# Output projection and second MLP product: from feature-major to token-major

## The chip, the cores and the metric

The kernel runs on one core of a Trainium2 chip. The metric is the device time of one execution in microseconds (us); the median of several runs is compared. A profiled execution gives the trace: when each instruction ran on each engine and what it waited for. PE is the matrix engine (TensorE), DVE the vector engine, ACT the scalar engine, POOL is GpSimd; SP issues the DMAs.

## The reference

Two layers of a hybrid block on 512 tokens x and 256 context tokens ctx, with D = 1024. A modulation vector of c (and of c_ctx) gives, per layer, shifts, scales and gates. A token mixer has three branches (a convolution over 31 tokens, a bidirectional mLSTM in chunks of 128, a latent attention with 8 heads). Their gated sum goes through the output projection. Then come a layer norm, an MLP with 4096 hidden features and a second layer norm:

```python
def layer_norm(x, g, b):
    mu = jnp.mean(x, -1, keepdims=True)
    var = jnp.mean(jnp.square(x - mu), -1, keepdims=True)
    return (x - mu) * lax.rsqrt(var + LN_EPS) * g + b

# per layer l, alpha = 4 ** 0.25
u = x * (1.0 + sc1) + sh1
y = (g_a * y_a + g_b * y_b + g_c * y_c) @ w_out[l] + b_out[l]
x = layer_norm(alpha * x + g1 * y, ln1_g[l], ln1_b[l])
x = layer_norm(alpha * x + g2 * sq_relu_mlp(x * (1.0 + sc2) + sh2, w1[l], b1[l], w2[l], b2[l]), ln2_g[l], ln2_b[l])
```

where sq_relu_mlp(u) = square(relu(u @ w1 + b1)) @ w2 + b2. In the first layer the 256 context tokens go through the same steps with their own modulation; in the second they only feed keys, values and states. The result is x, 512 x 1024.

## The kernel before

All activations lie feature-major: 128 features on the partitions, tokens along the free dimension (T = 768: 512 of x, then 256 of ctx; in the second layer only n = 512 are carried through the mixer's output and the MLP). A token tile tt is 128 tokens.

**Products.** `gemm` (L279) computes one tile of 128 output features. Its stationary operands are 128 x 128 blocks of the weight, its moving operand is the activation, 512 tokens and then 256. Each product is done three times (`mm3`, L265), as float32 in two halves: `wh` and `wl` of the weight (high part and rest), and likewise for the activation: h*h, h*l, l*h. The sum stands in `pg`, one of two PSUM buffers of two banks each; `gemm_parts` (L292) takes `pt`, of which there are four of one bank each.

**Weights.** `plan` (L201) lists all weight chunks (128 x 1024, 512 KB) in the order of use. `wget` (L249) hands out the next and stages two more: a DMA on SP's queue into `wr`, ACT casts it into `wh` (L261), DVE (for some chunks POOL) subtracts into `wl` (L262). There are three buffers of each.

**Order.** Only the first stage is written out by hand. After it the framework sets each engine's order when the program is built, earlier text first where several instructions are ready, so PE's work of a later step fills waits of an earlier one.

**Slots.** `slot` gives one of 35 general SBUF buffers of 128 x 768; `vp` has 12 buffers (vectors of attention and mLSTM, later `t1`), `mp` ("m") has 8 of 128 x 512.

**Output projection and first norm** (L1098 to L1107). The tokens go in groups of 256, `tg_`: three in layer 0, two in layer 1. Per group all eight chunks of w_out are loaded again; each output tile is multiplied by its gate and added to the residual (L1104), which came by DMA and an ACT scaling (`residual`, L1085). Then `ln_groups` (L304): for each token tile, eight PE transposes bring it to rows (L314), DVE takes mean and variance (L315 to L322, the power -0.5 on POOL, L321), ACT norms from PSUM (L326), and PE transposes each of the eight feature tiles back (L336) to `norm1` (L1074), which makes the MLP's input `u2` (scale and shift per feature on DVE, L1080; cast on ACT; rest on POOL, L1082) and, on ACT, the start value of the MLP's accumulator `acc` (L1083).

**MLP** (L1113 to L1141). Eight blocks f: four tiles of the first product with relu and square (L1126 to L1129), then, except in the last block, eight tiles of the second product, each with four k; DVE multiplies by the gate and adds into `acc` (L1139). The first two tiles and each block's last one are done in parts of 256 tokens (`split_spec`), so that they can start when one group is ready. In layer 0, `pull` (L346) also feeds in the next layer's modulation (L165, DVE).

**Last block and second norm.** `last_w2` (L1148) does the last block's second product per group of 256 and loads its four chunks for each; then the norm follows as above. In layer 0 `norm2` (L1160) makes the next layer's input u and stores the normed x feature-major; in layer 1 the rows are scaled by rows of ln2's weights (L1191, L1192, on DVE and POOL) and stored.

Layer 1's first products (`win`, L468) read u with 512 tokens at a time.

## Time and profile before

| | us |
|---|---|
| median of 3 runs | 2556.21 (2555.85 to 2561.79) |
| the profiled execution | 2557.35 |
| its span, first to last instruction | 2555.5 |

| engine | busy us | share | instructions |
|---|---|---|---|
| PE (matmul) | 2470.4 | 97% | 15272 |
| PE (weight load) | 2163.8 | 85% | 15272 |
| DVE | 1580.6 | 62% | 2847 |
| ACT | 939.5 | 37% | 1607 |
| POOL | 298.7 | 12% | 235 |

The granted TensorE clock was 0.993 of full speed. The stages, by the trace's own clock: in layer 0 the output projection runs from about 888 us, the MLP from 965, its last product from 1478; layer 1 begins at about 1525 and has them from 2130, 2180 and 2515.

How to read it: busy times are those of one execution. Matmuls are pipelined, so the time of one (0.39 us for 512 columns) is longer than the distance from one start to the next; what PE spends on one is read from starts in the timeline. "idle <- X" names what ended an engine's wait. The kernel lines (L266) are those of the kernel before; a helper's line stands for all its callers, and the tile names (pg<-zp) tell which.

### The profile page before, as it was taken

To read this page: it belongs to the slowest core of one execution; us is meant where nothing else is said; L and a number is where in the kernel's file an instruction comes from. 1 tells how busy PE (TensorE), PEld (TensorE's weight loads), DVE (VectorE), ACT (ScalarE), POOL (GpSimd) and SP (SyncE) were. 2 spreads that over 40 slices of the span, in tenths; PEclk is the share of its full clock that TensorE was granted. 3 is DMA by queue.
4 is the path that set the end of the run, shared out by engine and by line. 5 is a ranking of instruction groups with operands and counts; after the bars stand their busy time and mean duration, and the time that the engine had idled before them with its cause. 6 is when DMAs were issued, how large, how long until landed. Compare 5 with 4: busy or idle time off the path is not lost.

```text
span 2555.5 us, 38339 instructions
## 1 busy us (share of the span) xinstructions
PE 2470.4 (97%) x15272; PEld 2163.8 (85%) x15272; DVE 1580.6 (62%) x2847; ACT 939.5 (37%) x1607; POOL 298.7 (12%) x235
## 2 busy tenths in 40 slices
PE   7899989999999999999999999999999999999997
PEld 5888878888888899888888888977888888888887
DVE  4999976363356777655554379996043567554456
ACT  3123323222457563222222253333324575432323
POOL 0002132203000021000000031023411001100002
PEclk9999999999999999999999999999999999999999
DMA  7122344466110654343342252233563106333333
GB/s 264 53 75 70 98 163 161 166 195 210 62 34 1 188 168 142 122 131 115 108 129 88 65 149 78 59 106 101 175 203 111 50 18 213 101 99 92 99 94 113
DMA packets 137235, 298.45 MB, mean 117 GB/s; under 512 B 13776, under 2 KB 55248, under 8 KB 137056
## 3 DMA queue, kind: packets, MB, share of 16 engines
q1 hardware_dynamic: 137056, 296.00, 36.9%
q8 instruction: 120, 1.97, 0.3%
q14 instruction: 59, 0.48, 0.1%
HBM read 265.49 MB, written 30.46 MB: 116 GB/s over the span
## 4 chain that ended last, share of the span: by engine, by line
PE 81%; DVE 9%; DMA 4%; ACT 2%; issue 2%; POOL 1%; SPq 0%; DVEq 0%; ACTq 0%; POOLq 0%
PE pg L266 21%; PE pg L267 21%; PE pg L268 21%; PE pt L1003 2%; PE pt L982 2%; PE pt L266 2%; PE pt L267 2%; PE pt L268 2%; DVE ca L494 2%; DMA wm<-w_mod 1%; DMA ml<-z_dram 1%; PE pg L536 1%; PE pg L538 1%; PE pg L537 1%; DVE st L315 1%
## 5 line engine op out<-in xcount | busy, mean ns | idle before, releaser
L261 ACT CAST wh<-wr 128x1024 fp32r<-128x1024 f32 (+1 forms) x328 | 345.6, 1055 | 1202.4 <-PE pg L267 825.5
L262 DVE TENSOR_TENSOR wl<-wr,wh 128x1024 fp32r<-128x1024 f32 (+2 forms) x272 | 338.6, 1246 | 410.1 <-ACT wh L261 406.3
L268 PE MATMUL pg<-uh,wl 128*128 128x512 f32 (+1 forms) x1280 | 456.3, 356 | 2.2 <-DVE wl L262 2.2
L266 PE MATMUL pg<-uh,wh 128*128 128x512 f32 (+1 forms) x1280 | 457.2, 357 | 1.2 <-ACT gt__17278 L760 1.2
L267 PE MATMUL pg<-ul,wh 128*128 128x512 f32 (+1 forms) x1280 | 455.5, 356 | 0.7 <-POOL ul L1171 0.6
L266 PE MATMUL pg<-hidh,wh 128*128 128x512 f32 (+1 forms) x832 | 285.4, 344 | 3.9 <-DVE mv L318 2.0
L267 PE MATMUL pg<-hidl,wh 128*128 128x512 f32 (+1 forms) x832 | 284.9, 342 | 0.0
L268 PE MATMUL pg<-hidh,wl 128*128 128x512 f32 (+1 forms) x832 | 284.2, 342 | 0.0
L266 PEld LDWEIGHTS pg<-uh,wh 128*128 128x128 f32 x1280 | 244.2, 191 | 35.4 <-issue 2.5
L268 PEld LDWEIGHTS pg<-uh,wl 128*128 128x128 f32 x1280 | 243.9, 191 | 34.4 <-DVE wl L262 2.7
L267 PEld LDWEIGHTS pg<-ul,wh 128*128 128x128 f32 x1280 | 244.1, 191 | 33.2 <-POOL ul L1171 1.0
L494 DVE SCALAR_TENSOR_TENSOR ca<-hc,cols,ca 128x511 f32<-128x511 f32 (+9 forms) x360 | 227.8, 673 | 2.4
L262 POOL TENSOR_TENSOR wl<-wr,wh 128x1024 fp32r<-128x1024 f32 x56 | 145.7, 2602 | 562.6 <-ACT wh L261 562.6
L267 PE MATMUL pg<-u2l,wh 128*128 128x512 f32 (+1 forms) x608 | 210.3, 347 | 0.3 <-POOL u2l L1082 0.2
L1139 DVE SCALAR_TENSOR_TENSOR acc<-pg,mod,acc 128x512 f32<-128x512 f32 (+1 forms) x168 | 106.0, 659 | 168.6 <-PE pg L268 168.6
L268 PE MATMUL pg<-u2h,wl 128*128 128x512 f32 (+1 forms) x608 | 210.1, 347 | 0.0
L266 PE MATMUL pg<-u2h,wh 128*128 128x512 f32 (+1 forms) x608 | 209.9, 347 | 0.0
L165 DVE SCALAR_TENSOR_TENSOR mda<-wm,sil,mda 128x512 f32<-128x512 f32 x224 | 176.2, 808 | 7.6 <-DMA wm<-w_mod 5.0
L266 PEld LDWEIGHTS pg<-hidh,wh 128*128 128x128 f32 x832 | 157.3, 190 | 25.3 <-issue 3.5
L321 POOL TENSOR_TENSOR rs<-rs,mhalf 128x1 f32<-128x1 f32 x30 | 24.4, 819 | 1298.5 <-DVE rs L320 1298.5
L267 PEld LDWEIGHTS pg<-hidl,wh 128*128 128x128 f32 x832 | 157.9, 190 | 18.7 <-DVE hidl L1129 1.6
L268 PEld LDWEIGHTS pg<-hidh,wl 128*128 128x128 f32 x832 | 157.7, 189 | 18.0
(359 smaller groups left out, 4754.1 us busy)
## 6 DMA issues: line engine op xcount, KB each, us to landing
wr<-w SPq DMA_DIRECT2D x140, 512.0 KB, 3.6
wr<-w_in_fm SPq DMA_DIRECT2D x104, 512.0 KB, 3.8
wm<-w_mod SPq DMA_DIRECT2D x192, 256.0 KB, 4.5
wr<-w_out SPq DMA_DIRECT2D x40, 512.0 KB, 3.9
ml<-z_dram SPq DMA_DIRECT2D x104, 128.0 KB, 2.8
ml<-z_dram SPq DMA_DIRECT2D x48, 256.0 KB, 4.4
z_dram<-ml SPq DMA_DIRECT2D x32, 256.0 KB, 4.5
dm<-m_dram SPq DMA_DIRECT2D x20, 256.0 KB, 4.4
```

The lines of the kernel that those rows point to most:

```text
L165: ins = V.scalar_tensor_tensor(av[v], w, sil[:, k, v:v + 1], av[v], op0=OP.mult, op1=OP.add)
L261: A.copy(h[:, :n], r[:, :n])
L262: eng.tensor_sub(lo[:, :n], r[:, :n], h[:, :n])
L266: PE.matmul(ps, hs, xh, start=first, stop=False)
L267: PE.matmul(ps, hs, xl, start=False, stop=False)
L268: return PE.matmul(ps, ls, xh, start=False, stop=last)
L315: V.bn_stats(st[:, hf * 6:(hf + 1) * 6], ps)
L494: V.scalar_tensor_tensor(acc[:, a:b], h[:, a + d:b + d], wd(15 + d), acc[:, a:b], op0=OP.mult, op1=OP.add)
L536: PE.matmul(o, uh[:, t0:t0 + 128], wh[:, a:b], start=(k == 0), stop=False)
L982: PE.transpose(p2[:, y * 128:(y + 1) * 128], P[:, (k4 + y) * 128:(k4 + y + 1) * 128], ident)
L1003: PE.matmul(po[64 * i:64 * i + 64, :256], va[B_.k0 + k][:, h * 64:h * 64 + 64], B_.pts[i][k // 2][:, k % 2, :], start=(k == 0), stop=(k == ...
L1139: V.scalar_tensor_tensor(acc[mt][:, c0:c1], ps[:, c0:c1], mc[:, 40 + mt, v:v + 1], acc[mt][:, c0:c1], op0=OP.mult, op1=OP.add)
```

## The change

Output projection and second MLP product are computed with tokens on the partitions: 128 tokens of the activation are the stationary operand, 512 output features of the weight the moving one. Each token tile has two halves (hf) of 512 features, each in one PSUM bank. Tokens go in two groups, `tri`: three tiles each in layer 0 (the second is tiles 3, 4, 5, that is the last of x and both of ctx), two each in layer 1. The weights of w_out and w2 are packed accordingly, and are loaded twice (w_out, and w2's last block) where they were loaded three times in layer 0.

Gates, biases and residual scales, which were per partition, become rows of 1024, made once per layer on DVE, transposed, stored to DRAM and read back over all partitions (`rowv`, five buffers). Layer norm takes its statistics on the rows as they stand (`tok_norm`), without transposes ahead of it, and `tok_back` transposes the normed rows for the next product. The scale and shift behind that moves from DVE to ACT. The residual comes by rows and is scaled on POOL. The MLP's accumulator holds rows without gate and residual, in 12 buffers of `vp`; in blocks 1 to 6 POOL makes the second residual from the stored normed rows and writes it to DRAM, and after the seventh block DVE multiplies the accumulator by the gate's row and adds that residual. General slots go from 35 to 33, the PSUM tile `pg` from 768 to 1024 columns (two banks as before).

```diff
-    gp = ctx.enter_context(tc.tile_pool(name="gen", bufs=35))
+    gp = ctx.enter_context(tc.tile_pool(name="gen", bufs=33))
+    rp = ctx.enter_context(tc.tile_pool(name="row", bufs=5))
...
-        return pp.tile([128, T], F32, name="pg", tag="g", bufs=2)
+        return pp.tile([128, 1024], F32, name="pg", tag="g", bufs=2)
...
-            ng = 3 if l < L - 1 else 2
+            ng = 2
...
+        tri = [[0, 1, 2], [3, 4, 5]] if full else [[0, 1], [2, 3]]
+        split_spec = [(g[0] * 128, g[-1] * 128 + 128, 0) for g in tri]
...
+        def rowv(i):
+            t = rp.tile([128, 1024], F32, name="row", tag="row")
+            nc.sync.dma_start(t, v_dram[l, i:i + 1, :].to_broadcast([128, 1024]))
+            return t
...
         def norm1(k, c0, c1, ps):
...
-            V.tensor_scalar(uf[:, c0:c1], ps, up[:, k, v:v + 1], uq[:, k, v:v + 1], op0=OP.mult, op1=OP.add)
+            A.activation(uf[:, c0:c1], ps, AF.Identity, bias=uq[:, k, v:v + 1], scale=up[:, k, v:v + 1])
             A.copy(u2[k][0][:, c0:c1], uf[:, c0:c1])
             G.tensor_sub(u2[k][1][:, c0:c1], uf[:, c0:c1], u2[k][0][:, c0:c1])
-            A.activation(acc[k][:, c0:c1], ps, AF.Identity, bias=ab2[:, k, v:v + 1], scale=ag[:, k:k + 1])
...
+        def residual(tts):
+            res = {}
+            for tt in tts:
+                for hf in range(2):
+                    o = hf * 512
+                    r = res[tt, hf] = vt512("xr")
+                    if l:
+                        nc.sync.dma_start(r, n_dram[1, tt, hf])
+                        G.tensor_tensor(r, r, a1r[:, o:o + 512], op=OP.mult)
+                    else:
+                        nc.sync.dma_start(r, I["xt"][tt * 128:(tt + 1) * 128, o:o + 512])
+                        G.tensor_scalar(r, r, ALPHA, None, op0=OP.mult)
+                    G.tensor_tensor(r, r, b1r[kind(tt)][:, o:o + 512], op=OP.add)
+            return res
+        def tok_sums(tts, hf, ws, act, per, wide):
+            if wide:
+                pgs = [pg() for _ in range((len(tts) + 1) // 2)]
+                sums = [pgs[i // 2][:, i % 2 * 512:i % 2 * 512 + 512] for i in range(len(tts))]
+            else:
+                sums = [pt() for _ in tts]
+            n_k = per * len(ws)
+            for kp, get in enumerate(ws):
+                w = get()
+                for tt, ps in zip(tts, sums):
+                    for i in range(per):
+                        k = kp * per + i
+                        xh, xl = act(k, tt)
+                        mark[0] = mm3(ps, xh, xl, w[0][:, i * 512:i * 512 + 512], w[1][:, i * 512:i * 512 + 512],
+                                      k == 0, k == n_k - 1)
+            return sums
+        def tok_norm(tt, rows, dst):
...
+            for hf in range(2):
+                t = wtile("ln")
+                A.activation(t, rows[hf], AF.Identity, bias=rs[:, 1:2], scale=rs[:, 0:1])
+                if dst is not None:
+                    nc.sync.dma_start(dst[tt, hf], t)
+                ns.append(t)
+            return ns
+        def tok_back(tts, ns, emit):
+            for run in ([tt for tt in tts if tt < 4], [tt for tt in tts if tt >= 4]):
...
+                for k in range(8):
+                    ps = pt()
+                    for i, tt in enumerate(run):
+                        PE.transpose(ps[:, i * 128:(i + 1) * 128], ns[tt][k // 4][:, (k % 4) * 128:(k % 4 + 1) * 128], ident)
+                    emit(k, c0, c1, ps[:, :c1 - c0])
...
+        xr = residual(tri[0])
+        for gi, tts in enumerate(tri):
+            for hf in range(2):
+                ws = [lambda i=i: wget("w_out", l, hf * 4 + i) for i in range(4)]
+                sums = tok_sums(tts, hf, ws, z_of, 2, hf == 0)
+                for tt, ps in zip(tts, sums):
+                    t = vt512("t1")
+                    V.tensor_tensor(t, ps, g1r[kind(tt)][:, hf * 512:hf * 512 + 512], op=OP.mult)
+                    V.tensor_tensor(xr[tt, hf], xr[tt, hf], t, op=OP.add)
+            rows, xr = xr, residual(tri[gi + 1]) if gi + 1 < len(tri) else None
+            ns = {tt: tok_norm(tt, [rows[tt, 0], rows[tt, 1]], n_dram[0]) for tt in tts}
+            tok_back(tts, ns, norm1)
...
-                parts_f = split_spec if mt < 2 or last else [(c0, c1, c0) for c0, c1 in segs]
+                parts_f = split_spec if mt < 2 or last else None
...
             if f < NF - 1:
+                for hf in range(2):
...
+                    for tts in tri:
+                        sums = tok_sums(tts, hf, [lambda kp=kp: w2_of(kp) for kp in range(2)], h_of, 2, False)
+                        for tt, ps in zip(tts, sums):
+                            if f == 0:
+                                acc[tt, hf] = vt512("acc")
+                                A.copy(acc[tt, hf], ps)
+                            else:
+                                V.tensor_tensor(acc[tt, hf], acc[tt, hf], ps, op=OP.add)
+                        pull(1)
+            if 1 <= f <= 6:
+                for tt, hf in [(tt, hf) for tt in qts for hf in range(2)][2 * (f - 1):2 * f]:
+                    r = wtile("r2")
+                    o = hf * 512
+                    nc.sync.dma_start(r, n_dram[0, tt, hf])
+                    G.tensor_tensor(r, r, a2r[:, o:o + 512], op=OP.mult)
+                    G.tensor_tensor(r, r, b2r[kind(tt)][:, o:o + 512], op=OP.add)
+                    nc.sync.dma_start(r_dram[tt, hf], r)
+            if f == 6:
+                for tt in qts:
+                    for hf in range(2):
...
+                        nc.sync.dma_start(r, r_dram[tt, hf])
+                        V.tensor_tensor(acc[tt, hf], acc[tt, hf], g2r[kind(tt)][:, o:o + 512], op=OP.mult)
+                        V.tensor_tensor(acc[tt, hf], acc[tt, hf], r, op=OP.add)
...
+        def last_w2(tts):
+            for hf in range(2):
+                sums = tok_sums(tts, hf, [lambda kp=kp: wget("w2", l, NF - 1, hf * 2 + kp) for kp in range(2)], h_of, 2,
+                                hf == 0)
+                for tt, ps in zip(tts, sums):
+                    t = wtile("t2")
+                    V.tensor_tensor(t, ps, g2r[kind(tt)][:, hf * 512:hf * 512 + 512], op=OP.mult)
+                    V.tensor_tensor(acc[tt, hf], acc[tt, hf], t, op=OP.add)
...
-                V.tensor_scalar(uf[:, c0:c1], ps, np_[:, k, v:v + 1], nq_[:, k, v:v + 1], op0=OP.mult, op1=OP.add)
+                A.activation(uf[:, c0:c1], ps, AF.Identity, bias=nq_[:, k, v:v + 1], scale=np_[:, k, v:v + 1])
...
+            for tts in tri:
+                last_w2(tts)
+                ns = {tt: tok_norm(tt, [acc[tt, 0], acc[tt, 1]], n_dram[1] if tt < 4 else None) for tt in tts}
+                tok_back(tts, ns, norm2)
```

More of the change, by code (lines that the diff above doesn't have):

```diff
@@ L465, in build @@
         HB = lambda i: hbin[l][:, i:i + 1]
-        resid = I["xc"] if l == 0 else xs_dram
         def win(i, cols_n):
@@ L620, in build @@
             t = slot("kT")
-            A.activation(t, ps, AF.Identity, bias=kb[l][:, h:h + 1], scale=KSCALE)
+            A.activation(t, ps[:, :T], AF.Identity, bias=kb[l][:, h:h + 1], scale=KSCALE)
             kT.append(t)
@@ L1068, in build @@
                     V.tensor_sub(zz[mt][1], g, zz[mt][0])
-        parts = [(0, 0, S), (1, S, T)][:len(groups)]
-        acc = [None] * 8
         u2 = [None] * 8
@@ L1098, in build, with vt512 @@
-        xr = residual(*tg_[0][1:])
-        for gi, ((tts, v, c0, c1), zz) in enumerate(zip(tg_, zg)):
-            tp = [vp.tile([128, 512], F32, name="t1", tag="v") for _ in range(4)]
-            ts_ = [tp[k // 2][:, k % 2 * 256:(k % 2 + 1) * 256] for k in range(8)]
-            for mt in range(8):
-                ps = gemm(wget("w_out", l, mt), 0, 8, zz, [(0, 256, 0)])
-                V.scalar_tensor_tensor(ts_[mt], ps[:, :256], g1h[:, mt, v:v + 1], xr[mt], op0=OP.mult, op1=OP.add)
-            if gi + 1 < len(tg_):
-                xr = residual(*tg_[gi + 1][1:])
-            ln_fm(ts_, 8, [tts], norm1, c0)
+        def vt512(name):
+            return vp.tile([128, 512], F32, name=name, tag="v")
@@ new lines, in tok_norm @@
+        def tok_norm(tt, rows, dst):
+            st = small(12, "st")
+            for hf in range(2):
+                V.bn_stats(st[:, hf * 6:(hf + 1) * 6], rows[hf])
+            mv = small(2, "mv")
+            V.bn_aggr(mv, st)
+            rs = small(2, "rs")
+            V.tensor_scalar(rs[:, 0:1], mv[:, 1:2], EPS, None, op0=OP.add)
+            G.tensor_tensor(rs[:, 0:1], rs[:, 0:1], mhalf[:, 0:1], op=OP.pow)
+            V.scalar_tensor_tensor(rs[:, 1:2], mv[:, 0:1], -1.0, rs[:, 0:1], op0=OP.mult, op1=OP.mult)
+            ns = []
+            for hf in range(2):
[5 more added lines that the diff above has]
+            return ns
@@ L1112, in build @@
         FB, NF = 4, 8
+        acc = {}
+        a2r = rowv(9)
+        b2r = [rowv(7 + v) for v in range(nv)]
+        g2r = [rowv(5 + v) for v in range(nv)]
         for f in range(NF):
@@ L1182, in build @@
                     gb.append(t)
-            for gi, (gtt, v, c0, c1) in enumerate(tg_):
-                last_w2(v, c0, c1)
-                for tts, ns in ln_groups(acc, 8, [gtt], None):
-                    for tt, row in zip(tts, ns):
-                        for hf in range(2):
-                            o = hf * 512
-                            e1 = V if gi and hf == 0 else G
-                            e2 = V if gi else G
-                            e1.tensor_tensor(row[hf], row[hf], gb[hf][:, :512], op=OP.mult)
-                            e2.tensor_tensor(row[hf], row[hf], gb[2 + hf][:, :512], op=OP.add)
-                            nc.sync.dma_start(out[tt * 128:(tt + 1) * 128, o:o + 512], row[hf])
+            for gi, tts in enumerate(tri):
+                last_w2(tts)
+                for tt in tts:
+                    row = tok_norm(tt, [acc[tt, 0], acc[tt, 1]], None)
+                    for hf in range(2):
+                        o = hf * 512
+                        e1 = V if gi and hf == 0 else G
+                        e2 = V if gi else G
+                        e1.tensor_tensor(row[hf], row[hf], gb[hf][:, :512], op=OP.mult)
+                        e2.tensor_tensor(row[hf], row[hf], gb[2 + hf][:, :512], op=OP.add)
+                        nc.sync.dma_start(out[tt * 128:(tt + 1) * 128, o:o + 512], row[hf])
     ctx.close()
```

105 lines of the change are left out of this document (53 added, 52 removed).

## The prediction

> **What bounds the kernel now.** I read the page first, for which engine the end hangs on.
>
> ```profile
> span 2555.5 us, 38339 instructions
> ...
> PE 2470.4 (97%) x15272; PEld 2163.8 (85%) x15272; DVE 1580.6 (62%) x2847; ACT 939.5 (37%) x1607; POOL 298.7 (12%) x235
> ...
> PE 81%; DVE 9%; DMA 4%; ACT 2%; issue 2%; POOL 1%; SPq 0%; DVEq 0%; ACTq 0%; POOLq 0%
> ```
>
> PE is busy 97% of the span and carries 81% of the chain that ended last. Time is saved by giving PE less to do, and lost wherever PE is made to wait. Second came the busy time by stretch, for the three stages that the change touches in layer 0: attention's output and the output projection, the MLP, and the MLP's last product with its norm.
>
> ```profile
> 850.20:965.00 114.80, 112.72 (x851) 106.67 (x849) 85.89 (x168) 66.21 (x117) 20.67 (x28) 1.00 0.64 198
> 965.00:1477.50 512.50, 512.20 (x3245) 458.09 (x3246) 286.66 (x424) 130.88 (x185) 6.37 (x9) 1.00 0.35 111
> 1477.50:1542.00 64.50, 60.21 (x437) 54.18 (x436) 49.19 (x94) 40.60 (x70) 25.77 (x27) 1.00 0.47 139
> ```
>
> The columns are: length, then busy time of PE, weight loads, DVE, ACT and POOL, granted clock, DMA share, GB/s. PE idles 2.1, 0.3 and 4.3 us in them: both norms are already covered by matmuls of the next group of tokens. DVE is busy 56% of the MLP, ACT 26%, POOL 1%. The clock is full. So the change can win only PE work here, and there are hardly any waits to remove.
>
> **The matmuls.** Third came the timeline of PE, for the distance from one matmul to the next, since busy times of PE overlap.
>
> ```profile
> 1099.02 0.39 PE L266 MATMUL pg<-hidh,wh 128*128 128x512 f32 x1
> ...
> 1100.38 0.28 PE L266 MATMUL pg<-hidh,wh 128*128 128x256 f32 x1
> ...
> 1101.81 0.40 PE L266 MATMUL pg<-u2h,wh 128*128 128x512 f32 x1
> ```
>
> Six matmuls of 512 columns take 1100.38 - 1099.02 = 1.36 us, 0.2267 each; the twelve of 256 behind them take 1.43 us, 0.1192 each. Two of 256 cost 0.238: turning a pair into one of 512 saves 0.0117 us. The weights take the place of the moving operand, so every such product has 512 columns whatever the tokens. The number of columns stays; the number of matmuls falls. Output projection, layer 0: 8 output tiles x 8 k x 3 products x 3 groups = 576 of 256 become 288 of 512. Layer 1: 384 become 192. Second product of the MLP, layer 0, seven of eight blocks: each has 96 of 512 and 96 of 256, which become 144 of 512: 48 fewer, 336 in all. Last block: 288 become 144, in layer 1 192 become 96. Layer 1's other blocks are 96 of 512 before and after. That is 1056 matmuls fewer at 0.0117: **12.4 us**. Ten first-product tiles of layer 0 also go from three parts of 256 to two of 384.
>
> ```profile
> 699.69 0.34 PE L929 MATMUL pg<-wh,cgl 128*128 128x384 f32 x1
> ...
> 706.28 0.34 PE L928 MATMUL pg<-wl,cgh 128*128 128x384 f32 x1
> ```
>
> Between these lie 38 steps: 0.1734 each. 3 x 0.1192 - 2 x 0.1734 = 0.0108, times 10 x 24: **2.6 us**. Together 14.9 us (rounded down for the few records missing).
>
> From these rows a matmul costs about 12 ns beside its columns. The Trainium skill, "TensorE: Matmul & The Clock Gate", in the section "Wait — 56ns, not 53.3ns?", gives a fixed 2.5 ns per warm matmul; by it the 1296 matmuls would be worth an estimated 3 us. The trace has the durations, so the sum goes by the trace.
>
> **The transposes.** Rows that are already token-major need no turn ahead of the statistics.
>
> ```profile
> 1489.55 1.95 PE L314 MATMUL pt<-cst,acc 128*128 128x128 f32 x16
> 1491.25 0.36 PE L266 MATMUL pg<-hidh,wh 128*128 128x256 f32 x1
> ```
>
> Sixteen take 1.70 us of PE's time. There are ten such sets (three groups twice in layer 0, two twice in layer 1): 17.0 us. One stands in the tail, below; **15.3 us** come off. The turn back stays. Two new transposes for the row vectors cost 0.2.
>
> **The tail.**
>
> ```profile
> 2541.57 1.94 PE L314 MATMUL pt<-cst,acc 128*128 128x128 f32 x16
> 2546.54 0.69 DVE L1191 TENSOR_TENSOR ln<-ln,gb 128x512 f32<-128x512 f32 x1
> 2551.26 1.28 DVE L1192 TENSOR_TENSOR ln<-ln,gb 128x512 f32<-128x512 f32 x2
> ```
>
> Of the time from the last product to the first scaled row, 1.7 us are transposes. In their place come a multiply by the gate row and an add for the last tile, 0.7 each (next fence), 1.4. From the norm on all is as before: **0.3 us** less.
>
> **What DVE, ACT and POOL get.**
>
> ```profile
> L262 DVE TENSOR_TENSOR wl<-wr,wh 128x1024 fp32r<-128x1024 f32 x256 | 317.2, 1241 | 377.1 <-ACT wh L261 373.6 <-DMA ml<-z_dram 0.2
> L1139 DVE SCALAR_TENSOR_TENSOR acc<-pg,mod,acc 128x512 f32<-128x512 f32 x112 | 84.1, 751 | 168.6 <-PE pg L268 168.6
> L1139 DVE SCALAR_TENSOR_TENSOR acc<-pg,mod,acc 128x256 f32<-128x256 f32 x56 | 26.6, 475 | 0.0
> L315 DVE BATCH_NORM_STATS2 st<-pt 128x6 f32<-128x512 f32 x50 | 32.4, 677 | 21.3 <-PE pt L314 21.3
> L1128 DVE TENSOR_TENSOR r<-r 128x512 f32<-128x512 f32 x24 | 16.6, 692 | 0.6
> L326 ACT ACTIVATE ln<-pt,rs 128x512 f32<-128x512 f32 x50 | 35.3, 776 | 50.7 <-DVE rs L322 30.1 <-DVE rs L320 12.4 <-issue 6.4
> L666 ACT ACTIVATE dm<-dm,colg 128x128 f32<-128x128 f32 x80 | 24.6, 393 | 10.7 <-DVE dm L664 10.7
> L1126 ACT ACTIVATE r<-pt,cols 128x256 f32<-128x256 f32 x40 | 18.9, 472 | 23.9 <-PE pt L268 23.9
> L1081 ACT CAST u2h<-uf 128x256 fp32r<-128x256 f32 x40 | 16.4, 411 | 3.0 <-DVE uf L1080 2.9
> L806 POOL TENSOR_TENSOR ml<-ml 128x512 f32<-128x512 f32 x16 | 20.6, 1288 | 131.0 <-DMA z_dram<-ml 68.3 <-DMA wr<-w_in_fm 38.2 <-DVE ml L803 15.6
> ```
>
> Per block of layer 0, DVE did 8 x (0.751 + 0.475) = 9.8 us of accumulation; now it does 12 adds of about 0.7, 8.4 us (in the first block 12 ACT copies instead). After the seventh block come 24 multiplies and adds at 0.69, 17 us on DVE, beside 33 us of first products: hidden, since the weights of two tiles (16 us of PE) are staged ahead. Twelve weight chunks fall away, 1.24 us of DVE each. POOL gets 40 operations for the residual and 40 for the MLP's second residual, 103 us at 1.288; it was idle. SP's queue gets 60 transfers of 256 KB for that residual, 20 stores of normed rows and 15 rows spread over the partitions, against the twelve chunks of 512 KB saved: about 22 MB more in stages that ran at 111 to 198 GB/s. A store that waits for POOL holds the weight loads behind it, but a chunk lasts PE 36 x 0.2267 = 8 us, and two are staged ahead. If POOL were late by more, PE would wait: 0 to 6 us, I take **+1.0**.
>
> **Where PE will wait.** Two groups of three token tiles replace three of two, so each norm's chain is longer, and the fixed scale moves from DVE to ACT. (a) Layer 0's second norm, between its groups. Before, the last product summed in the pg buffers. Now its second half takes three pt buffers of four, just when the turn back of the first group holds them until ACT has read them. First turned tile: 0.7 + 0.7 + 0.7 for the third tile's multiply, add and statistics, about 1.5 for the small steps and the power, six normings of 0.7: 7 to 8 us behind the group's end. Each k then needs about 1.2 on ACT (scale and cast of 384, from 472 and 411 ns for 256). The second half is due at 36 x 0.2267 = 8.2 us and finds its buffers free only when ACT is through k = 4, at about 13 to 14. Between 0 (if the second half takes its buffers first) and 8: **+5.0**. (b) The end of that norm. Layer 1's first product reads 512 columns, and tile 3 now belongs to the second group. PE has nothing else: 7 to 8 us to the first turned tile, 1.3 for scale, cast and rest, then about 0.75 a k on ACT against 0.68 on PE. About 10 us idle.
>
> ```profile
> 1516.48 0.36 PE L266 MATMUL pg<-hidh,wh 128*128 128x256 f32 x1 [2.00 <-DVE mv L318]
> ```
>
> Before, the longest single wait there was these 2.00 us, and the stage's whole idle time 4.3, so **+5.5** (0 to 10). (c) Layer 0's first norm: the first halves of two tiles cover 48 x 0.1734 = 8.3 us, and tile 2's first 512 columns 5.4 more; u2 is whole after about 21. **+1.5** (0 to 5). (d) Layer 1's: the cover is as before, less the 1.7 us of transposes, which the chain lost too: **+0.5** (0 to 2). (e) The general pool goes from 35 to 33 slots. By the code, at the head tiles before the first merge 34 slots would be wanted (u 16, sa 8, head tiles 8, a gate tile, a temporary), so the last head's split waits until the first merge lets go of sa. A chain of about 4 us then stands ahead of part of the second merge, in each layer; a new order can also gain a little. -2 to 8: **+3.0**.
>
> **The sum.** -14.9 - 15.3 - 0.3 + 0.2 + 1.0 + 5.0 + 5.5 + 1.5 + 0.5 + 3.0 = -13.8. The profiled execution took 2557.35 us (2555.5 of span, 1.85 around it) and goes to 2543.5; it stood 1.1 above the median of the runs, 2556.21, so I forecast **2543** there, with 2533 to 2549 as this case's own range.
>
> **The rivals.** B: PE's waits in (a) to (e) are all covered, as those of before are. Then only -30.3 + 1 is left: about 2527, case range 2522 to 2533. For it: PE's order before is woven tightly, 0.3 us idle in 512. Against: (b) has no matmul to weave in. C: the waits come out near their ends. 8 + 10 + 5 + 2 + 8 + 1 = 34 against 30.3: 2549 to 2562, about even. For it: (a) and (b) rest on ACT, which also makes the weights' high parts in that stage. D, slower: DVE is late in draining the second product in layer 0. Three pt buffers of four are held; the first is wanted 6 matmuls into the next group and its sum ended 12 matmuls before this group's end, so DVE has 18 x 0.2267 = 4.1 us to add. There are 28 groups. Above an average wait of 0.5 us a group the gain is gone, above 0.8 the kernel is slower by over 0.3%; at 1.0 it gives 2571. For it: DVE works 56% of that stage in steps of 0.7 to 1.2, and POOL now runs beside it.
>
> ```profile
> 2547.27 3.46 DVE L1192 TENSOR_TENSOR ln<-ln,gb 128x512 f32<-128x512 f32 x2
> ...
> 2547.25 2.93 POOL L1191 TENSOR_TENSOR ln<-ln,gb 128x512 f32<-128x512 f32 x2 [0.93 <-ACT ln L326]
> ```
>
> Two adds that take 1.28 us alone took 3.46 while POOL read and wrote. The Trainium skill, "SBUF — State Buffer", section "Who interferes with whom", has it so: a DVE instruction with two operands in SBUF and POOL exclude each other; the trace agrees. Against D: even all 103 us of POOL fit into DVE's idle time of 225 in that MLP alone, and the adds have one operand in PSUM. E: a matmul costs by its columns alone, so merging saves nothing: 2543 + 15 = 2558, no change. Only the rows of the pitches speak to it, and against it.
>
> **How the numbers follow.** Forecast 0.60, B 0.12, C 0.16, D 0.10, E 0.02. A measurement of this kernel tells about 0.3%, 7.7 us, from no change. Faster takes the forecast and B, 0.72; no change C and E, 0.18; slower D, 0.10. The range 2527 to 2561 leaves out D and half of B.
>
> **What would show it.** PE's count should fall by about 1450, to 13,800, with no 256-column matmul on zp or hid and no transpose ahead of statistics. The first stretch should shrink by its 288 fewer matmuls and three sets of transposes; PE's idle time should be near 10 us ahead of layer 1's first matmul, named ACT, and some us in the last product's second half, named by a pt buffer's reader. Wrong would be: waits of PE on the accumulating adds (D), a pitch other than 0.227 with weights moving (E), or long waits in mLSTM or attention, which the sum leaves alone.

## The result and the profile after

| | before | after |
|---|---|---|
| median, us | 2556.07 (2555.85 to 2561.79) | 2580.03 (2576.88 to 2581.85) |
| profiled execution's span, us | 2555.5 | 2575.1 |

The ratio is 1.0088 [1.0072, 1.0104] (the interval is of 95%): slower by 0.9%. The forecast was 2543. The medians are 24.0 us apart, the two profiled executions only 19.6: the one of the kernel after was its fastest run.

The page of the kernel after, its first lines and the line of the chain:

```profile
span 2575.1 us, 35468 instructions
...
PE 2448.9 (95%) x13818; PEld 2096.5 (81%) x13818; DVE 1579.8 (61%) x2759; ACT 928.3 (36%) x1577; POOL 405.1 (16%) x317
...
PE 67%; issue 14%; DVE 9%; DMA 3%; ACT 3%; POOL 2%; SPq 0%; DVEq 0%; POOLq 0%; ACTq 0%
```

PE has 1454 instructions fewer and some 21 us less busy time, and the span is 19.6 us longer: PE stands still 41 us more (2575.1 - 2448.9 against 2555.5 - 2470.4). Its share of the chain fell from 81% to 67%, but nothing can be read from that: the chain has one piece of "issue" of 314 us from 2233.55 on, in layer 1's MLP, where PE is never idle, and in E7 below PE has 81% again.

To see where, I cut both executions at the same events: the first matmul of layer 0's output projection, the first of its second MLP product, the first of layer 1's first product, the same two in layer 1, and the last matmul of the last product. Busy time by stretch, before (columns as in the prediction):

```profile
878.31:998.55 120.24, 117.86 (x939) 113.46 (x938) 87.03 (x142) 73.23 (x126) 27.04 (x36) 1.00 0.56 173
998.55:1524.89 526.34, 522.64 (x3346) 467.84 (x3345) 297.29 (x455) 140.65 (x196) 14.77 (x13) 1.00 0.36 114
1524.89:2126.13 601.24, 588.57 (x3292) 502.48 (x3292) 377.08 (x739) 254.75 (x468) 106.81 (x70) 1.00 0.34 105
2126.13:2206.75 80.62, 78.34 (x617) 75.30 (x616) 53.50 (x90) 50.83 (x88) 19.38 (x20) 1.00 0.54 167
2206.75:2541.44 334.69, 333.69 (x1721) 284.95 (x1720) 169.45 (x215) 106.19 (x138) 10.27 (x8) 1.00 0.32 97
2541.44:2555.49 14.05, 2.07 (x19) 1.78 (x17) 9.59 (x17) 2.78 (x4) 6.75 (x7) 0.67 0.34 129
```

and after:

```profile
879.99:1002.10 122.11, 110.06 (x531) 93.66 (x529) 73.78 (x115) 57.32 (x96) 40.18 (x42) 0.94 0.51 169
1002.10:1527.74 525.64, 512.49 (x2666) 437.53 (x2666) 297.49 (x424) 145.52 (x192) 50.15 (x44) 0.99 0.40 131
1527.74:2132.06 604.32, 589.91 (x3275) 502.77 (x3275) 370.49 (x712) 254.30 (x474) 112.10 (x77) 0.99 0.33 108
2132.06:2225.24 93.18, 78.22 (x394) 64.97 (x393) 59.73 (x74) 46.49 (x76) 48.75 (x42) 0.89 0.54 180
2225.24:2553.82 328.58, 328.58 (x1610) 278.86 (x1608) 171.81 (x222) 109.53 (x145) 8.50 (x8) 1.00 0.34 112
2553.82:2575.09 21.27, 0.38 (x2) 0.00 (x0) 15.76 (x24) 4.13 (x6) 12.83 (x10) 0.56 0.26 99
```

Length minus PE's busy time is PE's idle time. In the two stages with a first norm it went from 2.4 to 12.1 us and from 2.3 to 15.0, in the stage with layer 0's second norm from 3.7 to 13.2, behind the last matmul from 12.0 to 20.9. POOL works 13 to 35 us longer in the three stages with norms. And the granted clock, 1.00 before, is 0.94, 0.99 and 0.89 there: beside the waits, matmuls at half clock are a loss of their own. One row of the waits of PE stands above all others (before's row, then after's; us in total, times, longest):

```profile
PE pt L336 <- ACT ln L326: 6.2, 9, 2.2
```

```profile
PE pt L1179 <- ACT ln L1164: 24.9, 9, 6.2
```

The turn back (the transposes of the normed rows to feature-major) waits for these rows: 24.9 us in nine waits, where before nine waits took 6.2.

The lengths of the stages, in us, from the same view of each kernel (E numbers as below):

| stage | before | after | E1 | E5 | E13 | E7 | E8 | E12 |
|---|---|---|---|---|---|---|---|---|
| ahead of it all | 878.3 | 880.0 | 878.0 | 879.0 | 881.7 | 878.4 | 880.8 | 880.7 |
| layer 0, projection, first norm | 120.2 | 122.1 | 117.3 | 117.0 | 120.9 | 110.7 | 113.6 | 111.4 |
| layer 0, MLP, second norm | 526.3 | 525.6 | 525.7 | 525.5 | 525.7 | 526.5 | 516.9 | 516.8 |
| layer 1, up to its projection | 601.2 | 604.3 | 604.2 | 601.2 | 604.7 | 602.0 | 602.6 | 603.2 |
| layer 1, projection, first norm | 80.6 | 93.2 | 98.7 | 91.1 | 87.3 | 84.9 | 84.9 | 82.8 |
| layer 1, MLP | 334.7 | 328.6 | 328.6 | 328.6 | 328.6 | 328.6 | 328.6 | 328.6 |
| behind the last matmul | 14.0 | 21.3 | 21.3 | 21.3 | 21.3 | 19.9 | 19.9 | 20.8 |

The first stage is the same work in all kernels after; it took 878.0 to 883.4. E6 and E14 leave layer 1's projection as it is and have 95.3 and 91.9 there, so differences of some 2 us in a stage are not read. The same holds for medians: that of the kernel before itself lay between 2556.1 and 2557.8 beside the different experiments.

### The profile page after: what moved, and what is told of

The parts are those of the page before. It is cut to its first block, busy times and chain, and to the rows that moved or that the text cites. A ratio compares the mean times of both kernels' runs of the same rounds, so it can differ in the third digit from the quotient of the medians.

```text
span 2575.1 us, 35468 instructions
## 1 busy us (share of the span) xinstructions
PE 2448.9 (95%) x13818; PEld 2096.5 (81%) x13818; DVE 1579.8 (61%) x2759; ACT 928.3 (36%) x1577; POOL 405.1 (16%) x317
## 4 chain that ended last, share of the span: by engine, by line
PE 67%; issue 14%; DVE 9%; DMA 3%; ACT 3%; POOL 2%; SPq 0%; DVEq 0%; POOLq 0%; ACTq 0%
PE pg L267 13%; PE pg L268 13%; PE pg L269 13%; PE pt L267 5%; PE pt L269 5%; PE pt L268 5%; PE pt L1039 2%; PE pt L1018 2%; DVE ca L498 1%; DMA wm<-w_mod 1%; PE pg L540 1%; PE pg L542 1%; PE pg L541 1%; DMA ml<-z_dram 1%; DVE wl L263 1%
## 5 line engine op out<-in xcount | busy, mean ns | idle before, releaser
L262 ACT CAST wh<-wr 128x1024 fp32r<-128x1024 f32 (+1 forms) x316 | 333.8, 1056 | 1171.2 <-PE pg L268 459.8
L263 DVE TENSOR_TENSOR wl<-wr,wh 128x1024 fp32r<-128x1024 f32 (+1 forms) x260 | 331.6, 1276 | 540.6 <-ACT wh L262 533.8
L267 PE MATMUL pt<-wh,hidh 128*128 128x512 f32 x600 | 234.8, 392 | 0.2 <-ACT uf L1287 0.2
L268 PE MATMUL pt<-wl,hidh 128*128 128x512 f32 x600 | 234.3, 390 | 0.0
L269 PE MATMUL pt<-wh,hidl 128*128 128x512 f32 x600 | 234.1, 390 | 0.0
L269 PE MATMUL pg<-u2h,wl 128*128 128x512 f32 (+1 forms) x528 | 188.2, 356 | 0.0
L267 PEld LDWEIGHTS pt<-wh,hidh 128*128 128x128 f32 x600 | 113.4, 189 | 23.6 <-ACT uf L1287 0.6
L269 PEld LDWEIGHTS pt<-wh,hidl 128*128 128x128 f32 x600 | 113.0, 188 | 23.8
L268 PEld LDWEIGHTS pt<-wl,hidh 128*128 128x128 f32 x600 | 113.1, 189 | 22.9
L267 PEld LDWEIGHTS pg<-u2h,wh 128*128 128x128 f32 x528 | 100.4, 190 | 18.5 <-ACT u2h L1110 3.2
L1246 DVE TENSOR_TENSOR acc<-acc,pt 128x512 f32<-128x512 f32 x120 | 80.0, 684 | 55.9 <-PE pt L269 55.9
```

The costliest lines, as they stand in the source:

```text
L262: A.copy(h[:, :n], r[:, :n])
L263: eng.tensor_sub(lo[:, :n], r[:, :n], h[:, :n])
L267: PE.matmul(ps, hs, xh, start=first, stop=False)
L268: PE.matmul(ps, hs, xl, start=False, stop=False)
L269: return PE.matmul(ps, ls, xh, start=False, stop=last)
L1246: V.tensor_tensor(acc[tt, hf], acc[tt, hf], ps, op=OP.add)
```

## The experiments

Each is the kernel after with the edit named, if nothing else is said; ratios are to the kernel before. Four theories stood: T1, the tiles that were to cover the turn back stand behind it; P, POOL's new work (Theory 2 in the first expectations); G, the groups of 3 + 3; C, the clock.

### E1, E2, E4 and B1: the cover

The first two tiles of w1 moved from the pg buffers to pt with the change. The turn back takes a pt buffer eight times, once for each k, and stands first in the text, so the tiles get theirs only behind it. In PE's order after, the row behind the last product is the turn back itself, five transposes after 4.94 us of nothing:

```profile
954.43 0.39 PE L269 MATMUL pt<-wh,zp 128*128 128x512 f32 x1
959.76 1.53 PE L1179 MATMUL pt<-cst,ln 128*128 128x128 f32 x5 [4.94 <-ACT ln L1164]
964.22 0.79 PE L267 MATMUL pg<-u2h,wh 128*128 128x512 f32 x1 [2.94 <-ACT u2h L1110]
```

E1 (e1_cover) puts them back:

```
-  if parts_f:
-      sums = gemm_parts(w, 8, u2, parts_f)
+  if mt < 2:
+      ps = gemm(w, 0, 8, u2, [(c0, c1, 512 * i) for i, (c0, c1, _) in enumerate(split_spec)])
...
```

> The changed kernel, with the first two tiles of the first product summed in a pg buffer again (each group in its own bank) instead of in pt buffers. Theory 1, lost cover: the turn back of the last group takes the pt buffers first, so the first halves of these two tiles cannot stand ahead of it, and PE waits 8.4 us at the end of layer 0's first norm (5.1 + 3.3) and 7.5 us at layer 1's (6.4 + 1.1). With pg they stand ahead again: the time falls by 12 to 18 us against the changed kernel, to 2562 to 2568, and the two waits go below 2 us each. Theory 2, POOL's queue: these waits come from the norm's own chain being longer, whatever PE has to do: under 4 us gained. Theory 3, the weights as the moving operand are slower: no change.

Measured: 2576.66, 1.0073 [1.0058, 1.0088], only 3.4 us better: by the number alone Theory 2 was right. In layer 0 Theory 1 held: the first halves now follow the product without a gap, and the stage is 4.8 us shorter:

```profile
954.41 0.39 PE L269 MATMUL pt<-wh,zp 128*128 128x512 f32 x1
954.63 0.33 PE L267 MATMUL pg<-u2h,wh 128*128 128x384 f32 x1
```

In layer 1 the stage became 5.5 us longer, by a wait that nobody had on the list; DVE and POOL there:

```profile
2204.23 11.72 DVE L263 TENSOR_TENSOR wl<-wr,wh 128x1024 fp32r<-128x1024 f32 x1 [16.12 <-ACT wh L262]
```

```profile
2202.44 2.52 POOL L1256 TENSOR_TENSOR r<-r,row 128x512 f32<-128x512 f32 x2
...
2212.39 2.50 POOL L1256 TENSOR_TENSOR r<-r,row 128x512 f32<-128x512 f32 x2
```

A weight subtraction that takes 1.24 us took 11.72: it ends 1.06 us after POOL's ten operations for the MLP's residual, which ran back to back, had ended at 2214.89. PE waited 3.70 us for these weights, where E1's cover was to be:

```profile
2216.01 0.58 PE L269 MATMUL pt<-u2h,wl 128*128 128x256 f32 x1 [3.70 <-DVE wl L263]
```

So long a hold is the exception: of the 260 subtractions in the kernel after itself none took more than 2.38 us.

B1 (b1_before_pt) does the same harm to the kernel before, by one condition:

```
-  if last:
+  if mt < 2 or last:
       sums = gemm_parts(w, 8, u2, parts_f)
```

> The kernel before, with one part of the change alone: the first two tiles of the first product summed in pt buffers. Theory 1: the lost cover is a cost by itself and has nothing to do with the token-major products. In layer 1 PE then waits some 5 to 8 us at the end of the first norm, where no other product has its tokens ready; in layer 0 less, since tile 2's first 512 columns belong to groups that are ready: 6 to 12 us over the kernel before, 2562 to 2568. Theories 2 and 3: within 3 us of the kernel before.

Measured: 2570.34, 1.0047 [1.0031, 1.0064]: 12.6 us slower, somewhat beyond the expected range. The two stages with a first norm are 3.7 and 5.7 us longer (124.0 and 86.3); the other 3.9 us of that profile are in the first stage, which the edit leaves alone. T1 is shown from this side.

E2 (e2_pow_first) writes the next group's residual behind the norm in the text, E4 (e4_three) does this with E1 and sums layer 1's second halves in pg.

> The changed kernel, with the next group's residual written behind the norm of the group before it instead of ahead, so that POOL's power of the norm no longer stands behind eight to twelve residual operations. Theory 2, POOL's queue: the waits in the middle of the second group (2.55 and 1.14 us in layer 0, 4.77 and 0.57 us in layer 1) go below 1 us each, and the half clock behind two of them goes too: 8 to 13 us less than the changed kernel, 2567 to 2572. Theory 1, lost cover alone: these waits stay at the places where the transposes stand in PE's order, under 3 us gained.

> Both edits before, and in layer 1 also the second half of each group's product summed in pg instead of pt, so that it need not wait for the turn back of the group before it (1.85 and 0.62 us of waits). If the three causes are separate and add up, the time is 2545 to 2556; the end of layer 0's second norm (5.1 + 3.3 us) and its pt waits (about 4 us), which none of the three touches, stay. If the waits only move to what is late next, it stays above 2560.

Measured: E2 2580.74, 1.0088 [1.0073, 1.0103]; E4 2575.78, 1.0068 [1.0053, 1.0083]. Text order did not move POOL's order: the residual's operations, ready earlier, still stood ahead of the power. E2 thus says nothing of P. E4's third part was worth under 1 us, too little to be read.

### E5 and E13: POOL, its queue and the rest

E5 (e5_no_pool) gives both residuals' row operations to DVE:

```
-  G.tensor_scalar(r, r, ALPHA, None, op0=OP.mult)
-  G.tensor_tensor(r, r, b1r[kind(tt)][:, o:o + 512], op=OP.add)
+  V.scalar_tensor_tensor(r, r, ALPHA, b1r[kind(tt)][:, o:o + 512], op0=OP.mult, op1=OP.add)
...
-  G.tensor_tensor(r, r, a2r[:, o:o + 512], op=OP.mult)
+  V.tensor_tensor(r, r, a2r[:, o:o + 512], op=OP.mult)
...
```

> Both residuals' row operations on DVE instead of POOL; the rest as in the kernel after. Theory P (POOL's three residual operations of about 1.29 us stand ahead of the norm's power in its queue, and lock DVE's subtractions with two SBUF operands out): the waits between the groups of the two first norms (2.55 and 1.14 us at 918 to 925, 4.77 and 0.57 at 2161 to 2166) and the half-clock stretches behind them mostly go, some 9 us of waits and 8 us of slow steps: 2562 to 2570. Rival (the waits come from the order of the tiles alone, POOL is as quick as DVE for this): the waits stay and DVE has 56 us more: 2578 to 2584.

Measured: 2565.39, 1.0026 [1.0016, 1.0036]: 14.6 us better, within the range of Theory P. The row operations are 48.7 us on DVE, but its busy time rose by only 11.9 (1579.8 to 1591.7), as its other operations no longer run beside POOL's. The two first-norm stages lose 5.1 and 2.1 us (the second too little to be read alone), and the stage between, in which I had looked for nothing, 3.1: there PE's waits for DVE's merges (`ml`) fell from 2.6 to 0.6 us. P is shown, and more than one mechanism is in it. The first is POOL's queue. The kernel after in layer 1, POOL, DVE and PE:

```profile
2159.48 1.35 POOL L1125 TENSOR_TENSOR xr<-xr,row 128x512 f32<-128x512 f32 x1 [43.12 <-PE pg L269]
2160.91 1.28 POOL L1129 TENSOR_TENSOR xr<-xr,row 128x512 f32<-128x512 f32 x1
2162.14 1.26 POOL L1125 TENSOR_TENSOR xr<-xr,row 128x512 f32<-128x512 f32 x1
2163.36 0.56 POOL L1159 TENSOR_TENSOR rs<-rs,mhalf 128x1 f32<-128x1 f32 x1
```

```profile
2163.96 1.21 DVE L1160 SCALAR_TENSOR_TENSOR rs<-mv,rs 128x1 f32<-128x1 f32 x1 [4.29 <-POOL rs L1159]
```

```profile
2166.07 1.11 PE L1179 MATMUL pt<-cst,ln 128*128 128x128 f32 x4 [4.61 <-ACT ln L1164]
```

The power, 0.56 us, stands behind three row operations; DVE, ACT and then PE (4.61 us idle) stand behind the power. E13 (e13_pool_late) changes only this: with E2's order of the text, a dependency puts the second group's residual behind the powers, all of it still on POOL.

```
+  if power[0] is not None:
+      tc.add_manual_dep(i.ins, power[0].ins.name, NOSYNC)
```

> The kernel after with one order set on POOL: the second group's residual operations stand behind the norm's three (two) powers; all of them stay on POOL. Theory Q (the loss to POOL is its queue: the power waits behind three residual operations, 3.9 us in layer 1): the waits 2.55 + 1.14 and 4.77 + 0.57 us between the groups go as they did with the operations on DVE, some 9 us and the slow steps behind them, 2566 to 2572. Theory S (the loss is the lockout: POOL's operations with two operands in SBUF stop DVE's subtractions and adds whenever they run): the waits stay about as they are, as the operations now run beside DVE's normings, or others come: 2576 to 2584.

Measured: 2573.28, 1.0062 [1.0044, 1.0080]: 6.8 us better, between the two theories. In the same place:

```profile
2159.48 1.55 POOL L1163 TENSOR_TENSOR rs<-rs,mhalf 128x1 f32<-128x1 f32 x1 [41.83 <-DVE rs L1162]
2161.36 0.56 POOL L1163 TENSOR_TENSOR rs<-rs,mhalf 128x1 f32<-128x1 f32 x1 [0.34 <-DVE rs L1162]
2161.89 3.59 POOL L1127 TENSOR_TENSOR xr<-xr,row 128x512 f32<-128x512 f32 x2
```

```profile
2163.12 1.21 DVE L263 TENSOR_TENSOR wl<-wr,wh 128x1024 fp32r<-128x1024 f32 x1
```

The wait of 4.61 us is gone and the stage 5.8 us shorter. But the row operations now run beside DVE's work (two take 3.59 us with a subtraction of DVE among them, where two of the rows above take 2.6), the last turn back comes later (longest wait of a turn back 6.8 us instead of 6.2), and layer 0 gains only 1.2 us. So of POOL's 14.6 us the queue is about 7; the rest is what goes only when POOL does none of it.

### E6 and E14: the stretch behind the last matmul

DVE and POOL in the kernel after, behind PE's last matmul at 2553.82:

```profile
2553.39 1.27 DVE L1276 TENSOR_TENSOR t<-pg,row 128x512 f32<-128x512 f32 x2
2554.59 2.34 DVE L1277 TENSOR_TENSOR acc<-acc,t 128x512 f32<-128x512 f32 x2
2556.86 1.28 DVE L1276 TENSOR_TENSOR t<-pt,row 128x512 f32<-128x512 f32 x2
2558.05 3.44 DVE L1277 TENSOR_TENSOR acc<-acc,t 128x512 f32<-128x512 f32 x2
2561.42 1.86 DVE L1154 BATCH_NORM_STATS2 st<-acc 128x6 f32<-128x512 f32 x3
```

```profile
2556.35 2.93 POOL L1310 TENSOR_TENSOR ln<-ln,gb 128x512 f32<-128x512 f32 x2
2559.24 3.37 POOL L1311 TENSOR_TENSOR ln<-ln,gb 128x512 f32<-128x512 f32 x2
```

Not one tile's gate and add are left there, as I had reckoned, but all four, first half included, since DVE was held by the other group's norm. Two pairs of adds take 2.34 and 3.44 us in place of 1.28: POOL is scaling the other group's rows.

E6 (e6_tail) scales and shifts all last rows on DVE (`e1 = e2 = V`):

> Only the last norm's scale and shift by rows, all on DVE instead of shared with POOL. Theory P: the steps behind PE's last matmul grew from 16.3 to 25.7 us because the last group's DVE operations ran beside POOL's and took 2.3 to 3.4 us for two in place of 1.28; with POOL idle there the end comes 3 to 8 us sooner: 2572 to 2577. Rival (the tail is longer because three tiles stand in the last group of rows instead of two and DVE now has all the work): as long or longer, 2580 to 2584.

Measured: 2578.39, 1.0074 [1.0059, 1.0089]. The stretch is 1.2 us shorter (20.1): what POOL no longer blocks, DVE now does itself. The expected 3 to 8 us did not come; the median lies between the two ranges. The rival's reason does not hold either, for in layer 1 both groups have two tiles.

E14 (e14_no_gate) leaves the gate out of the last block:

```
-  V.tensor_tensor(t, ps, g2r[kind(tt)][:, hf * 512:hf * 512 + 512], op=OP.mult)
-  V.tensor_tensor(acc[tt, hf], acc[tt, hf], t, op=OP.add)
+  V.tensor_tensor(acc[tt, hf], acc[tt, hf], ps, op=OP.add)
```

> The kernel after with the gate's multiply by rows left out of the last block (each sum is added as it is; eight multiplies in layer 1 and twelve in layer 0 fewer). Theory: the steps behind PE's last matmul, 7 us longer than in the kernel before, are DVE's queue for the last group: four multiplies of 0.64, four adds of up to 1.7 and statistics, all behind PE's end; without the multiplies the end comes 2.5 to 4 us sooner, and layer 0's second norm some tenths: 2574 to 2578. Rival (what stands behind PE's end is the norm's chain through POOL and ACT, whatever DVE has to add): within 1 us of the kernel after, 2579 to 2581.

Measured: 2569.31, 1.0044 [1.0028, 1.0060]: 10.7 us less, far more than I expected. The stretch is 5.0 us shorter, and layer 0's second norm as much (520.6):

```profile
2552.49:2568.78 16.29, 0.39 (x2) 0.00 (x0) 7.48 (x15) 2.93 (x4) 9.31 (x9) 0.64 0.30 113
```

So the gate by rows is 5 of the 7.2 us. In the kernel before it was one fused operation of DVE with a scalar per partition; by rows it is a multiply and an add, with the add's both operands in SBUF. E14 takes away both prices: the multiplies, and with the sum read from PSUM the adds behind PE's end take 0.69 us each beside POOL, where two took up to 3.44. Of what is left, the power is a part again, behind POOL's rows:

```profile
2558.35 0.16 DVE L1160 SCALAR_TENSOR_TENSOR rs<-mv,rs 128x1 f32<-128x1 f32 x1 [3.77 <-POOL rs L1159]
```

### E7 and E8: the edits together, and the groups

E7 (e7_all) is E1, E5, E6 and pg for layer 1's second halves together; E8 (e8_groups) also changes layer 0's groups:

```
-  tri = [[0, 1, 2], [3, 4, 5]] if full else [[0, 1], [2, 3]]
+  tri = [[0, 1, 2, 3], [4, 5]] if full else [[0, 1], [2, 3]]
```

with norms, and the other blocks' second product, by pairs of tiles.

> The first two w1 tiles summed in the other PSUM pool, layer 1's second half too, residuals on DVE, the last rows on DVE. If the parts add up: first tiles -3.4 (measured), POOL -10 to -18, tail -3 to -8: 2552 to 2564. What is left by this theory is the end of layer 0's second norm (5.1 + 3.3 us of wait and 5.3 us of slow steps) and the third tile of each group. If the waits only move to the next place that is short: 2570 to 2576.

> As the kernel with the four edits, and layer 0's tokens in groups of four and two tiles for the two products, norms by pairs. Theory (the group of 3 + 3 takes away the cover at the end of layer 0's second norm, as tile 3 of layer 1's first 512 columns is in the second group): the wait of 5.1 + 3.3 us there and its slow steps of 5.3 go, about -10 to -13 beside the kernel with four edits alone, 2542 to 2554. Rival (the last pair's norm is as late for PE, whichever tiles it holds): within 3 us of that kernel.

Measured: E7 2552.67, 0.9976 [0.9964, 0.9988]; E8 2548.80, 0.9963 [0.9949, 0.9977]. Alone the parts gave 3.4, 14.6 and 1.6 us; together 27.4. With POOL out of the way (E5) the cover shortens both first-norm stages, from 117.0 to 110.7 and from 91.1 to 84.9; alone (E1) it shortened only layer 0's. That the weights were what failed it in layer 1 fits the 11.72 us above. Layer 0's second norm was untouched by E7 and lost 9.5 us in E8, as G has it (E7's row, then E8's):

```profile
989.10:1515.55 526.45, 512.68 (x2667) 437.77 (x2666) 310.69 (x449) 145.46 (x192) 13.46 (x20) 0.99 0.40 131
```

```profile
994.42:1511.35 516.93, 509.62 (x2666) 429.09 (x2665) 312.79 (x447) 140.97 (x189) 11.65 (x19) 1.00 0.40 133
```

E7's waits at the end of this norm, 4.91 and 2.92 us, are gone in E8; in their place stand waits of 5.0 us in all on buffers that ACT has still to read. The whole gained less, 3.9, as the first norm gave 2.9 back and the first stage ran 2.4 longer.

### E9: filling the waits

E9 (e9_fill) lets PE do work that nobody reads where it waits:

> The kernel after with PE work added that nobody reads: 22 matmuls of 512 columns (5.0 us) behind the last group's sums of layer 0's two norms, 28 (6.3 us) of layer 1's first, and 28 transposes (3.1 us) behind the turn back at the end of layer 0's two norms. 14 us of the 22.5 us are meant to lie in waits, those of the second norm mostly in the turn back of its first group. Theory C (the clock falls to half because PE stood still some us, and the 21.5 us of slow steps are a price of the waits on top of the waits): where the fill takes a wait's place the half-clock stretches behind it go, slow steps fall to 8 to 12 us and the whole by about as much, 2566 to 2572, although PE has 22 us more to do. Rival (the clock falls for another reason, or the slow steps hide under the chains anyway): 2578 to 2590.

Measured: 2587.56, 1.0113 [1.0099, 1.0127]: outside Theory C's range and within the rival's. The three stages grew by 4.6, 5.1 and 4.5 us for 22.5 us of fill, so some 8 lay in waits, not 14: the transposes meant for the second wait came behind it. For the clock the place where the fill did sit is what counts. The kernel after, at the end of layer 0's first norm:

```profile
944.00:954.70 10.70, 10.70 (x48) 8.63 (x46) 7.66 (x10) 2.11 (x2) 2.52 (x3) 1.00 0.53 155
...
958.75:968.99 10.24, 6.30 (x19) 4.38 (x20) 1.83 (x8) 8.91 (x22) 4.14 (x9) 0.50 0.67 236
968.99:979.00 10.01, 10.01 (x60) 9.18 (x59) 0.00 (x0) 7.28 (x19) 6.14 (x9) 1.00 0.42 130
```

and with 22 matmuls in its first wait:

```profile
955.00:968.56 13.56, 10.69 (x49) 8.45 (x48) 7.60 (x19) 5.60 (x8) 1.63 (x3) 1.00 0.68 234
968.56:971.97 3.41, 3.41 (x17) 3.41 (x17) 0.00 (x0) 3.41 (x13) 2.22 (x6) 0.50 0.67 227
```

```profile
959.79 5.15 PE L1154 MATMUL pg<-wh,zp 128*128 128x512 f32 x22
964.89 0.66 PE L1190 MATMUL pt<-cst,ln 128*128 128x128 f32 x4
968.41 0.81 PE L1159 MATMUL pg<-cst,ln 128*128 128x128 f32 x3 [2.87 <-ACT ln L1175]
```

The clock no longer falls at the first wait, which the 22 matmuls fill; it falls behind the second, of 2.87 us, for 3.41 us instead of 10.24. So the half clock follows PE's waits. In the three stages together it lasted 34 us instead of 51, and the slow steps cost some 12 us instead of 16. That is some 4 us less, where the fill made the three stages 14 us longer: that filling pays was not shown.

### E10, E11 and E12: two more repairs

On E8: E10 (e10_early) takes layer 1's residual for both groups ahead of the first, since in E8 DVE stood still for its load and SP issued it behind eight weights:

```profile
2141.98 0.69 DVE L1126 TENSOR_TENSOR xr<-xr,row 128x512 f32<-128x512 f32 x1 [2.42 <-DMA xr<-n_dram]
```

E11 (e11_fine) does layer 1's last product tile by tile, each weight chunk once; E12 (e12_best) is both.

> The kernel of groups of four and two with, in layer 1, the residual of all four token tiles loaded and scaled ahead of the first group instead of behind it. Theory: the wait of 1.2 + 5.9 us at the first turn back of layer 1 comes from DVE standing still 2.4 us for the second group's residual, whose loads stand behind eight weight loads in SP's queue, and from its 5.2 us of row operations ahead of the norm's scale; with the rows early the wait and the slow steps behind it (3.2 us) mostly go: 5 to 9 us less than that kernel, 2540 to 2544. Rival (the turn back is late for the normings on ACT anyway): within 2 us of it.

> The kernel of groups of four and two with layer 1's last product tile by tile: each weight chunk once for all four token tiles, each tile's gate, norm and rows behind its own sum. Theory: the 7 us by which the steps behind PE's last matmul grew are DVE's queue for a whole group (two tiles' gate, add and statistics behind the other group's rows); with one tile last the end comes 3 to 6 us sooner than in that kernel, 2543 to 2546. Rival (DVE's work for four tiles is the same in sum and only comes later): as long or up to 3 us longer.

> Both: layer 1's residual early and its last product tile by tile. If the two add up: 2535 to 2540, 0.7 to 0.9% below the kernel before; if both rivals hold, 2547 to 2552.

Measured: E10 2547.66, 0.9956 [0.9941, 0.9971]; E11 2549.70, 0.9961 [0.9945, 0.9976]; E12 2545.96, 0.9951 [0.9939, 0.9964]. The rivals of E10 and E11 held. In E10 the wait (5.7 us in E8's trace) went, but another came (2.2 us on a weight's low part), and the stage is only 1.0 us shorter. In E11 the end is 0.9 us later: DVE's work is the same in sum, and PE is not what it waits for. E12 lies 1 us below the range for both rivals and 6 above the one for both theories. It beats the kernel before by 0.5% and the kernel after by 1.3%.

## Why the prediction was wrong, point by point

The sum's terms by stage: -7.0, -2.8, -5.1, -2.8 and -0.3 for the five that the change touches (layer 0's projection; its MLP; layer 1's projection; its MLP; the end), and +4.2 that had no place. Measured: +1.9, -0.7, +12.6, -6.1, +7.2, and +4.8 in the other two stages.

These sizes overlap with those of single experiments below and do not add up with them.

**Matmuls and transposes: right.** 512 columns with the weight moving took 0.2267, twelve steps here:

```profile
939.70 0.39 PE L267 MATMUL pt<-wh,zp 128*128 128x512 f32 x1
...
942.42 0.39 PE L267 MATMUL pt<-wh,zp 128*128 128x512 f32 x1
```

The trace has 1056 rows of 512 columns and 480 of 384 more than before, and 2832 of 256 and 160 transposes fewer; at the pitches of the prediction's rows that is 32 us less, as the sum had it (14.9 + 15.3, and 1.7 for the set in the tail). Rival E is out. Layer 1's MLP gained 6.1 where 2.8 was forecast, which is luck: 25 steps of PE in the kernel before were together 2.8 us longer than their pitch there, and none is in the kernel after.

**(b), the end of layer 0's second norm: right; (a), between its groups: too high.** I had +5.5 for (b) and +5.0 for (a); PE's idle time grew by 5.2 and by 2.0. That the whole stage's grew by 9.5, near my 10.5, is in part luck: the other 2.3 us are six waits of 0.39 us in the MLP for `modrows` (the transposes of the next layer's modulation), which the sum did not have. At the end of the norm stood 4.92 and 2.94 us, named ACT, near the 10 that I gave:

```profile
1523.28 1.53 PE L1179 MATMUL pt<-cst,ln 128*128 128x128 f32 x5 [4.92 <-ACT ln L1164]
1527.74 0.79 PE L267 MATMUL pg<-uh,wh 128*128 128x512 f32 x1 [2.94 <-ACT uh L1288]
```

The cause of (b) was right as well: with tile 3 in the first group these two waits are gone (E8 against E7). E8 also norms by pairs, and what this alone does was not tried.

**(c), layer 0's first norm: failed.** "The first halves of two tiles cover 48 x 0.1734 = 8.3 us" took for granted that PE does them there. They were in the diff, in another buffer pool, and the pool decides the order. +1.5 became 9.7 us of idle time. B1 shows the cause by itself. It is not the only one: with the cover back (E1) the stage still idles 6.1 us more than before, and only with POOL's work gone as well (E7) does it idle for 2.0 us, against 2.4 in the kernel before.

**(d), layer 1's: failed worst.** "The cover is as before" was wrong for the same reason (B1: 5.7 us), and the power behind POOL's row operations came on top (E13: 5.8 us): +0.5 became 12.7.

**POOL: failed.** "103 us at 1.288; it was idle" was right in the amount (106 us more) and wrong in what it costs: +1.0 became about 14.6 (E5). I compared totals. What counts is that a 0.56 us power on the critical chain shares POOL's queue (E13), and that DVE's operations with both operands in SBUF take longer beside POOL's: 3.44 us for two adds of 1.28, up to 2.38 us for a subtraction of 1.24, and once 11.72 (E1). How much of the 14.6 is this second part was not measured by itself. I had quoted the row that shows the lock and used it only inside rival D.

**The end: failed.** -0.3 became +7.2. I counted one tile's gate and add behind the last matmul, and it was a group's: E14.

**The clock: not in the sum.** At half clock a step of 512 takes 0.42 to 0.43 instead of 0.2267; over such stretches in the three norm stages PE's steps were some 16 us longer, where before there was none. It is a price on top of the waits, which the sum had at nothing.

**(e), the slots:** I allowed +3.0. The first stage is within its scatter, and layer 1's 3.1 us went with POOL's work (E5), so nothing is left for the slots. Rival D had the right sign and the wrong place: no wait of PE on the accumulating adds was found. C had the right kind in (c) and (d) alone, whose waits came above its upper ends of 5 and 2.

Open: how much of the loss the clock alone is (E9 did not separate it); what of POOL's second half is the lock and what the mere load; why layer 1's projection in E12, 82.8, is still 7.3 us above the 75.5 that the sum has for it.

## What to carry to other kernels

Before counting on a cover, follow which buffers it takes and who is ahead of it in them: moving a product to another pool moves its place in the order. A small operation on the critical chain makes its engine a critical one; give that engine no bulk work, however idle it is in total. Price each wait of the matrix engine above its own length, since the clock may fall behind it; test edits alone and together, for their gains do not add up.

## What the runs showed of the hardware

DVE against POOL: one subtraction with two operands in SBUF held for 11.72 us, until a run of ten operations of POOL was through. The Trainium skill, "SBUF — State Buffer", section "Who interferes with whom", says that these exclude each other; the trace agrees. Here DVE did not get its turn between two of POOL's operations; in E13 it did, with a subtraction of 1.21 us between two that took 3.59. What decides this, no run here shows.

The half clock came in stretches of 3.41, 6.8 and 10.24 us. The Trainium skill, "TensorE: Matmul & The Clock Gate", section "What's actually happening", has PE judged idle or busy over free-running windows of about 3.4 us; one, two and three such windows agree with the stretches. A single wait need not be that long: here 2.87 us was enough, behind four transposes (E9). Cut into windows of 3.41 us, the sixteen traces (from 360 us to 25 us before the end) say more: every window at full clock in which PE was busy for less than 1.47 us was followed by half clock, and some with more were (the kernel after, 1501.47 to 1504.88: busy 1.54 us, no wait above 1.37). The full clock came back only behind windows with 2.90 us or more. So several short waits close together cost the clock as one long wait does.
